# Last layer's middle norm: residual turned inside the last y group, next weights in places of their own, first token tile's products ahead of the second tile's norm

## The chip, the cores and the metric

The kernel runs on one NeuronCore of a Trainium2 chip. Its engines run side by side and wait for each other by semaphores: PE (TensorE, matrix products and transposes into PSUM), DVE (VectorE), ACT (ScalarE), POOL (GpSimd) and SP, which here issues DMA transfers. The metric is device time in microseconds (us); lower is better.

## The reference, cut to what matters

A two-layer backbone: 256 tokens, width 1024, float32. Layer 0 mixes by attention, layer 1 by a state-space scan (SSD); each is followed by a norm, a squared-ReLU MLP of width 4096 and another norm. The change lies in layer 1, at the norm between mixer and MLP:

```
y_lat = finish(z_l, x_l, yl_f, flip(yl_b))            # ends in  y @ w_out   (2048 -> 1024)
h_lat = layer_norm(ALPHA*h_lat + g_m_l*y_lat, ln_mix_g[i], ln_mix_b[i])
f_lat = squared_relu_mlp(h_lat*(1 + sc_f_l) + sh_f_l, ff_w1[i], ff_w2[i])
h_lat = layer_norm(ALPHA*h_lat + g_f_l*f_lat, ln_ff_g[i], ln_ff_b[i])
```

## The kernel before

**Precision.** Every large product keeps float32 precision by splitting both operands into a high and a low part and adding three products (h·h, l·h, h·l). Weights come from memory as float32 in transfers of 1 MB (`raw`, two buffers, `emit_w`, L47 to L62), each holding two units. For each unit ACT casts the high half (`wh`, two casts of 128x512, L61) and DVE subtracts to get the low half (`wl`, L62). Only four `wh`/`wl` pairs exist (pool `wsp`), so a cast waits until PE has read the unit four places earlier, and a transfer waits until both units of the `raw` two places earlier are converted. `next_w` emits up to two units ahead.

**Order.** A scheduler of the tile framework places the instructions: inside each engine they may stand in another order than the source writes them. The engine then works through its list in that order. SP's list holds nearly all transfers.

**The stage of the change** is the second half of `layer1` (L1007 on). The SSD runs in four groups of heads; the last, `ssd(3)`, is woven with `so()`, the products of w_out for blocks k = 0 to 11. The products for k = 12 to 15 follow after the group, tile of 128 tokens by tile (`i`), half of 512 columns by half (`h`): 12 matmuls each, four sets, in the PSUM tiles so00, so01, so10, so11. The residual lies transposed in `X[0]`; 16 PE transposes (`xr`, L1060) and four ACT copies turn it into `Xt`, here between the halves. `add_half` (L277) multiplies by the gate, adds and takes the half's statistics on DVE; `ln_mid` (L298) forms the moments, normalises the tile in one DVE instruction (L302), turns it back with 8 PE transposes (`ut`, L308) and splits it into `u4h` and `u4l` for each of the eight k blocks.

Then comes the MLP. The first four of its 32 hidden blocks are computed with tokens as rows (`f1r`, 24 matmuls of 512 columns for each token tile, over weight units 140 to 143), relu and square (`rr`), and four transposes back (`rt`, L383). The others (`f1a`, 24 matmuls of 256 columns for each block) go the usual way. The second product `f` (w2, `down`) follows after each eight blocks. Three PSUM banks, "aux", serve xr, ut, f1r, rt and f1a in turn. The two rows of the norm's gain and bias (`mixg`, `mixb`) and the two of the last norm (`ffg`, `ffb`) are broadcast transfers of 512 KB; ACT scales the first two (L1097), DVE applies them to `Xt` (L1102).

Of the kernel before, what the change touches and what calls it, by code (L numbers as in the profile page):

```python
# [39 lines left out]
class Net:  # L40
# [217 lines left out]

    def row(self, r, nm):

        t = self.tk.tile([128, 1024], F32, tag="row", name=nm, bufs=4)
        self.nc.sync.dma_start(t, self.a["rows"][r, :].partition_broadcast(128))
        return t

    def down(self, acc, lh, ll, w, k, last, tiles=(0, 1), halves=(0, 1)):

        mm = self.nc.tensor.matmul
        wh, wl = w
        for i in tiles:
            for h in halves:  # L270
                c = slice(512 * h, 512 * h + 512)
                ps = acc[i][h]
                mm(ps, lh(i), wh[:, c], start=(k == 0), stop=False)  # L273
                mm(ps, ll(i), wh[:, c], start=False, stop=False)  # L274
                mm(ps, lh(i), wl[:, c], start=False, stop=last)  # L275

    def add_half(self, acc, i, h, g, x, st):  # L277

# [19 lines left out]
    def ln_mid(self, i, x, st, aff, uh, ul):  # L298

        nc = self.nc  # L300
        mv = self.moments(st, f"lm1{i}")
        nc.vector.tensor_scalar(x, x, mv[:, 0:1], mv[:, 1:2], op0=ALU.subtract, op1=ALU.mult)  # L302
        c = slice(128 * i, 128 * i + 128)
        for q in range(2):
            pt = self.bank("aux", f"ut{i}{q}")
            for m in range(4):
                k = 4 * q + m
                nc.tensor.transpose(pt[:, 128 * m:128 * m + 128], x[:, 128 * k:128 * k + 128], self.ident)  # L308
            for m in range(4):
                k = 4 * q + m  # L310
                p = pt[:, 128 * m:128 * m + 128]
                sc, sh = aff[:, 0, k:k + 1], aff[:, 1, k:k + 1]
                nc.scalar.activation(uh[k][:, c], p, AF.Identity, bias=sh, scale=sc)
# [5 lines left out]
                nc.vector.tensor_sub(ul[k][:, c], t, uh[k][:, c].bitcast(F32))  # L319

    def ln_out(self, i, x, st, g, b):
        nc = self.nc
# [52 lines left out]
    def hidden_rows(self, i, ps, fs):  # L375
# [4 lines left out]
        nc.vector.tensor_mul(r, r, r)  # L380
        pt = self.bank("aux", f"rt{i}")
# [490 lines left out]
    def ssm_in(self, g, uh, ul):  # L872
# [19 lines left out]
        xw = [sp.tile([128, 2, 512], F32, tag=f"xw{d}", name=f"xw{g}{d}") for d in range(2)]  # L892
# [119 lines left out]
    def layer1(self):  # L1012
# [9 lines left out]
        self.sT = self.cst.tile([128, 2, 192], F32, name="sT")  # L1022
        self.aneg = self.cst.tile([128, 1], F32, name="aneg")
        nc.scalar.activation(self.aneg, self.vec("alog"), AF.Exp)
        with tc.tile_pool(name="dq", bufs=1, space=DRAM) as dqp:
            dq = dqp.tile([2, 64, 256], F32, name="dq")
            self.dq = dq
            with tc.tile_pool(name="sp", bufs=2) as sp:
                self.sp = _Multi(tc, sp, dict(cy=2, ct=1, B=1, C=2, xt0=2, xt1=2, xw0=1, xw1=1, Bt=1, xc=1,
                                              cf=2, cb=2, S0=1, S1=1, A=2, E=2, W=2))  # L1030
                for j in range(NZ):
                    self.z_tile(j, uh, ul)
# [4 lines left out]
                acc = [[self.bank("mm", f"so{i}{h}") for h in range(2)] for i in range(2)]  # L1037
                st = lambda y, k: (lambda i: y[k % 8][:, 256 * (k // 8) + 128 * i:256 * (k // 8) + 128 * i + 128])

                def so():  # L1040
                    for k in range(12):
                        self.down(acc, st(yh, k), st(yl, k), self.next_w(whole=True), k, False)
                        yield
                self.weave(self.ssd(3, yh, yl), so())
        aff = self.affine("affm1", self.vec("mixg")[:, 8:16], self.vec("mixb")[:, 8:16], (0,),
                          mT[:, :, 32:40], mT[:, :, 24:32])
        u4h, u4l = self.new_act("u4")
        with tc.tile_pool(name="tk", bufs=1) as self.tk, tc.tile_pool(name="fp1", bufs=2) as fp:
            X = self.tk.tile([128, 2, 1024], F32, name="Xt")
            ws = [self.next_w(whole=True, ahead=0) for _ in range(4)]  # L1050
            bn = [self.stat_tile(f"bm{i}") for i in range(2)]
            for i in range(2):
                for h in range(2):
                    for k in range(12, 16):
                        self.down(acc, st(yh, k), st(yl, k), ws[k - 12], k, k == 15, (i,), (h,))
                    if h == 0:
                        for q in range(2):
                            pt = self.bank("aux", f"xr{i}{q}")
                            for m in range(4):
                                nc.tensor.transpose(pt[:, 128 * m:128 * m + 128],  # L1060
                                                    self.X[0][:, 4 * q + m, 128 * i:128 * i + 128], self.ident)
                            nc.scalar.copy(X[:, i, 512 * q:512 * q + 512], pt)
                    self.add_half(acc, i, h, self.gates[2], X[:, i, :], bn[i])
                self.ln_mid(i, X[:, i, :], bn[i], aff, u4h, u4l)

            self.fp = _Multi(tc, fp, dict(fh=9, fl=9, r=2, q=2))
            pair = lambda m: tuple(self.fp.tile([128, 256], F32R, tag=t, name=f"f1{t}{m}") for t in ("fh", "fl"))
            ws = [self.next_w(whole=True) for _ in range(4)]
            first = [pair(m) for m in range(4)]
            for i in range(2):  # L1070
                ps = self.bank("aux", f"f1r{i}")
                c = slice(128 * i, 128 * i + 128)
                for k in range(8):
                    wh, wl = (w[:, 512 * (k % 2):512 * (k % 2) + 512] for w in ws[k // 2])
                    nc.tensor.matmul(ps, u4h[k][:, c], wh, start=(k == 0), stop=False)
                    nc.tensor.matmul(ps, u4l[k][:, c], wh, start=False, stop=False)
                    nc.tensor.matmul(ps, u4h[k][:, c], wl, start=False, stop=(k == 7))
                self.hidden_rows(i, ps, first)
            acc = [[self.bank("mm", f"f1{i}{h}") for h in range(2)] for i in range(2)]
            ag, ab = self.row(2, "mixg1"), self.row(3, "mixb1")  # L1080
            fg, fb = self.row(4, "ffg1"), self.row(5, "ffb1")
            for c in range(4):
                fs = [] if c else list(first)
                for m in range(len(fs), 8):
                    w = self.next_w()
                    fh, fl = pair(m)
                    ps = self.bank("aux", f"f1a{m}")[:, :256]
                    self.gemm(ps, w, u4h, u4l, 0, 256)
                    self.hidden(ps, 0, 256, fh, fl)
                    fs.append((fh, fl))  # L1090
                lh = lambda m: (lambda i: fs[m][0][:, 128 * i:128 * i + 128])
                ll = lambda m: (lambda i: fs[m][1][:, 128 * i:128 * i + 128])
                for m in range(8 if c < 3 else 4):
                    self.down(acc, lh(m), ll(m), self.next_w(whole=True), 8 * c + m, False)
                if c == 1:
                    for t in (ag, ab):
                        nc.scalar.activation(t, t, AF.Copy, scale=ALPHA)  # L1097
                    for i in range(2):
                        for t, op in ((ag, ALU.mult), (ab, ALU.add)):
                            for h in range(2):  # L1100
                                x = X[:, i, 512 * h:512 * h + 512]
                                nc.vector.tensor_tensor(x, x, t[:, 512 * h:512 * h + 512], op=op)  # L1102
            ws = [self.next_w(whole=True) for _ in range(4)]
            bn = [self.stat_tile(f"bf{i}") for i in range(2)]
            for i in range(2):
                for h in range(2):
                    for m in range(4, 8):
                        self.down(acc, lh(m), ll(m), ws[m - 4], 24 + m, m == 7, (i,), (h,))
                    self.add_half(acc, i, h, self.gates[5], X[:, i, :], bn[i])
                self.ln_out(i, X[:, i, :], bn[i], fg, fb)  # L1110

    def chain(self, *gs):
        for g in gs:
# [96 lines left out]
```

## Time and profile before

| what | value |
|---|---|
| time, three runs | 1177.57, 1180.91, 1181.55 us; median 1180.91 |
| the profiled execution | 1180.05 us; its span 1178.3 us, so 1.75 us lie around the span |
| PE busy | 1120.6 us (95%), 6976 matmuls; weight loads 911.6 us (77%) |
| DVE, ACT busy | 838.2 us (71%), 603.3 us (51%) |
| chain that ended last | PE 80%, DVE 8%, DMA 6%, ACT 5% |

Times in the rows below are microseconds from the start of the span. "Busy" says nothing by itself about what a wait costs; in this stage it matters which wait ends last before PE goes on. Ends of matmuls are modelled, so the distance between starts is their rate.

### The profile page before, as it was taken

How to read it: one execution, taken by the hardware profiler on the slowest of the kernel's cores; microseconds unless marked ns; L12 is line 12 of the kernel's file. 1: busy time of each engine (PE TensorE's matmuls, PEld its weight loads, DVE VectorE, ACT ScalarE, POOL GpSimd, SP SyncE). 2: the span in 40 equal slices, each digit the busy share in tenths (PEclk: the TensorE clock that was granted, in tenths of full speed). 3: DMA queues.
4: the chain of work that ended last, by engine and by line, in shares of the span. 5: the costliest groups of instructions: out<-in, count | busy, mean ns of one | idle time of the engine just before them, and what ended most of it. 6: DMA issues, size and time to landing. Idle time of an engine off the chain costs nothing.

```text
span 1178.3 us, 18541 instructions
## 1 busy us (share of the span) xinstructions
PE 1120.6 (95%) x6976; PEld 911.6 (77%) x6976; DVE 838.2 (71%) x1701; ACT 603.3 (51%) x1382; POOL 48.2 (4%) x79
## 2 busy tenths in 40 slices
PE   6999999998999999999999898999999996999996
PEld 4777767977978878878898776767777675898895
DVE  4499885867949667764435888979897768565566
ACT  4377776145422312322314647787878856454551
POOL 1200000022000000000001400000000000000000
PEclk8999999998999999999999999999999998999998
DMA  8833342522636466752322125435455563455551
GB/s 326 310 126 125 108 145 87 173 100 74 202 118 221 148 209 225 256 192 72 107 72 73 53 105 153 152 108 179 145 168 150 199 214 112 175 183 195 195 179 72
DMA packets 41433, 182.79 MB, mean 155 GB/s; under 512 B 4608, under 2 KB 5248, under 8 KB 28288
## 3 DMA queue, kind: packets, MB, share of 16 engines
q1 hardware_dynamic: 41056, 181.36, 45.9%
q8 instruction: 55, 0.90, 0.3%
q10 hardware_dynamic: 288, 0.26, 0.1%
q14 instruction: 34, 0.28, 0.1%
HBM read 180.41 MB, written 1.18 MB: 154 GB/s over the span
## 4 chain that ended last, share of the span: by engine, by line
PE 80%; DVE 8%; DMA 6%; ACT 5%; issue 1%; SPq 0%; DVEq 0%; ACTq 0%
PE f0a L87 5%; PE f0a L88 5%; PE f0a L89 5%; PE f0b L87 5%; PE f0b L89 5%; PE f0b L88 5%; PE y L983 3%; PE f L275 2%; PE f L274 2%; PE f L273 2%; PE f1a L89 2%; PE f1a L87 2%; PE f1a L88 2%; PE q L78 2%; DMA wm<-in_w_mod 2%; PE x L89 2%
## 5 line engine op out<-in xcount | busy, mean ns | idle before, releaser
L61 ACT CAST wh<-raw 128x512 fp32r<-128x512 f32 x404 | 237.8, 620 | 392.9 <-PE f0b L88 125.9
L62 DVE TENSOR_TENSOR wl<-raw,wh 128x512 fp32r<-128x512 f32 x404 | 268.5, 687 | 118.5 <-ACT wh L61 117.6
L87 PE MATMUL f0a<-u1h,wh 128*128 128x512 f32 (+1 forms) x320 | 112.7, 354 | 1.5 <-ACT u1h L193 1.5
L87 PE MATMUL f0b<-f0fh,wh 128*128 128x512 f32 (+1 forms) x320 | 113.8, 356 | 0.0
L89 PE MATMUL f0a<-u1h,wl 128*128 128x512 f32 (+1 forms) x320 | 112.1, 351 | 0.0
L88 PE MATMUL f0a<-u1l,wh 128*128 128x512 f32 (+1 forms) x320 | 112.0, 352 | 0.0
L89 PE MATMUL f0b<-f0fh,wl 128*128 128x512 f32 (+1 forms) x320 | 111.7, 349 | 0.0
L88 PE MATMUL f0b<-f0fl,wh 128*128 128x512 f32 (+1 forms) x320 | 110.9, 347 | 0.1
L150 DVE SCALAR_TENSOR_TENSOR ma<-wm,cs,ma 128x1024 f32<-128x1024 f32 x70 | 88.7, 1281 | 22.4 <-DMA wm<-in_w_mod 22.3
L87 PEld LDWEIGHTS f0a<-u1h,wh 128*128 128x128 f32 x320 | 61.6, 193 | 11.8 <-ACT u1h L193 2.3
L89 PEld LDWEIGHTS f0b<-f0fh,wl 128*128 128x128 f32 x320 | 60.2, 188 | 10.4 <-issue 2.1
L87 PEld LDWEIGHTS f0b<-f0fh,wh 128*128 128x128 f32 x320 | 60.1, 188 | 10.4 <-issue 2.6
L89 PEld LDWEIGHTS f0a<-u1h,wl 128*128 128x128 f32 x320 | 61.8, 193 | 8.0 <-issue 0.4
L88 PEld LDWEIGHTS f0b<-f0fl,wh 128*128 128x128 f32 x320 | 60.1, 188 | 9.6 <-issue 1.4
L88 PEld LDWEIGHTS f0a<-u1l,wh 128*128 128x128 f32 x320 | 61.6, 193 | 7.7 <-issue 0.4
L87 PE MATMUL f1a<-u4h,wh 128*128 128x256 f32 x224 | 63.5, 284 | 0.0
L89 PE MATMUL f1a<-u4h,wl 128*128 128x256 f32 x224 | 63.4, 283 | 0.0
L88 PE MATMUL f1a<-u4l,wh 128*128 128x256 f32 x224 | 63.4, 283 | 0.0
L87 PE MATMUL x<-u2h,wh 128*128 128x512 f32 x128 | 51.2, 400 | 2.2 <-DVE cy L794 2.2
L967 ACT ACTIVATE W<-A,sT 128x128 f32<-128x128 f32 (+1 forms) x128 | 50.2, 458 | 5.7 <-DMA A<-dq 3.1
L89 PE MATMUL x<-u2h,wl 128*128 128x512 f32 x128 | 51.2, 401 | 0.3 <-DVE wl L62 0.3
L361 DVE SCALAR_TENSOR_TENSOR X<-f0b,mT,X 128x256 f32<-128x256 f32 x48 | 21.0, 478 | 42.8 <-PE f0b L89 42.8
(435 smaller groups left out, 2724.8 us busy)
## 6 DMA issues: line engine op xcount, KB each, us to landing
raw<-in_wall SPq DMA_DIRECT2D x102, 1024.0 KB, 5.0
wm<-in_w_mod SPq DMA_DIRECT2D x96, 512.0 KB, 4.4
A<-dq SPq DMA_DIRECT2D x32, 256.0 KB, 4.5
E<-dq SPq DMA_DIRECT2D x32, 256.0 KB, 4.9
X<-in_xT SPq DMA_DIRECT2D x8, 256.0 KB, 8.3
gate<-in_rows SPq DMA_DIRECT2D x2, 512.0 KB, 12.8
out_dram<-Xt SPq DMA_DIRECT2D x4, 256.0 KB, 2.0
mixg<-in_rows SPq DMA_DIRECT2D x1, 512.0 KB, 5.9
```

Source lines behind the costliest of these rows:

```text
L61: nc.scalar.copy(h, src[:, c])
L62: nc.vector.tensor_sub(l, src[:, c], h.bitcast(F32))
L78: self.mm = lambda *a, **k: self.tc.keep_in_program_order(self.nc.tensor.matmul(*a, **k))
L87: mm(ps, wh[:, k, :], ah[k][:, c0:c1], start=(k == 0), stop=False)
L88: mm(ps, wh[:, k, :], al[k][:, c0:c1], start=False, stop=False)
L89: mm(ps, wl[:, k, :], ah[k][:, c0:c1], start=False, stop=(k == 7))
L150: nc.vector.scalar_tensor_tensor(t, wm, c, t, op0=ALU.mult, op1=ALU.add)
L273: mm(ps, lh(i), wh[:, c], start=(k == 0), stop=False)
L274: mm(ps, ll(i), wh[:, c], start=False, stop=False)
L275: mm(ps, lh(i), wl[:, c], start=False, stop=last)
L967: nc.scalar.activation(W[:, h, o:o + l1 - l0], A[:, h, l0:l1], AF.Relu, scale=-1.0, bias=self.sT[:, st, r + h:r + h + 1])
L983: mm(ps[64 * a:64 * a + 64, l0:l1], lh[:, hc:hc + 64], mv, start=(n == 0), stop=(n == 5))
```

## The change

Five edits, all around the middle norm of layer 1:

1. The 16 transposes of the residual and their copies move into `so()`, four after each of the odd k from 5 to 11, into a tile that takes the place of `xw` (which gets a pool of its own).
2. The first three of the four weight units of the token-row products (140 to 142) get places of their own, six buffers of the tag "row", and are converted before the norms. The fourth is taken as usual, after the last split of tile 0.
3. The token-row products of tile 0 stand in the source before `ln_mid` of tile 1.
4. Their transposes `rt` follow later, after hidden blocks 4 and 5.
5. The four row transfers move behind the second product of the second eight blocks in the source; they use the "row" places that the weights leave.

The core of the diff:

```
-        t = self.tk.tile([128, 1024], F32, tag="row", name=nm, bufs=4)
+        t = self.tk.tile([128, 1024], F32, tag="row", name=nm, bufs=6)
...
+    def res_rows(self, x, i, q):
+        pt = self.bank("aux", f"xr{i}{q}")
+        for m in range(4):
+            nc.tensor.transpose(pt[:, 128 * m:128 * m + 128], self.X[0][:, 4 * q + m, 128 * i:128 * i + 128], self.ident)
+        nc.scalar.copy(x[:, 512 * q:512 * q + 512], pt)
...
+                        if k % 2 and k > 3:
+                            i, q = divmod((k - 5) // 2, 2)
+                            self.res_rows(X[i], i, q)
...
+            for n in range(3):
+                wh, wl = (self.tk.tile([128, 1024], F32R, tag="row", name=f"f1w{n}{p}", bufs=6) for p in "hl")
+                self.emit_w(self.wpos, [(wh[:, 512 * q:512 * q + 512], wl[:, 512 * q:512 * q + 512]) for q in range(2)])
...
-                self.ln_mid(i, X[:, i, :], bn[i], aff, u4h, u4l)
+                if i:
+                    with tc.issue_after(turned[0].ins), tc.issue_after(turned[1].ins):
+                        first_w.append(self.next_w(whole=True, ahead=0))
+                    rows.append(f1_rows(0))
+                turned = self.ln_mid(i, X[i], bn[i], aff, u4h, u4l)
+            rows.append(f1_rows(1))
...
+                    if c == 0 and m < 6:
+                        self.rows_turn(m - 4, rows[m - 4], first)
```

What this does to the engines' lists, at three places. **PE, from the end of so11.** Before, tile 1's transposes (ut10, ut11) stood ahead of every f1r product; names end in running numbers:

```order
L275 MATMUL so11_9136<-wl139_9600,yh7_6515 128x512
L308 MATMUL ut10_9747<-con_78,Xt_9590 128x128 x4
L308 MATMUL ut11_9768<-con_78,Xt_9590 128x128 x4
L1075 MATMUL f1r0_9839<-wh140_9791,u4h0_9568 128x512
L1076 MATMUL f1r0_9839<-wh140_9791,u4l0_9576 128x512
```

Now tile 0's transposes follow the last so11 product, and tile 1's stand inside tile 0's products:

```order
L1091 MATMUL f1r0_9782<-f1w0l_9634,u4h1_9598 128x512
L1089 MATMUL f1r0_9782<-f1w1h_9641,u4h2_9599 128x512
L1090 MATMUL f1r0_9782<-f1w1h_9641,u4l2_9607 128x512
L1091 MATMUL f1r0_9782<-f1w1l_9642,u4h2_9599 128x512
L1089 MATMUL f1r0_9782<-f1w1h_9641,u4h3_9600 128x512
L316 MATMUL ut10_9815<-con_78,Xt1_9538 128x128 x2
L1090 MATMUL f1r0_9782<-f1w1h_9641,u4l3_9608 128x512
```

So ten products of tile 0 no longer wait for the second norm. **DVE, from the last weight unit of w_out (139) to the normalisation of tile 0**, now (before, no weight unit stood between wl139 and that normalisation, `Xt<-Xt,lm10mv`):

```order
L62 TENSOR_TENSOR f1w0l_9634<-raw140_9635,f1w0h_9633 128x512 x2
L62 TENSOR_TENSOR f1w1l_9642<-raw140_9635,f1w1h_9641 128x512 x2
L290 TENSOR_TENSOR gt00_9677<-so00_9136,gate2_90 128x512
L291 TENSOR_TENSOR Xt0_9381<-Xt0_9381,gt00_9677 128x512
L290 TENSOR_TENSOR gt01_9693<-so01_9137,gate2_90 128x512
L292 BN_STATS bm0_9663<-Xt0_9381 128x6
L62 TENSOR_TENSOR f1w2l_9648<-raw142_9649,f1w2h_9647 128x512 x2
L291 TENSOR_TENSOR Xt0_9381<-Xt0_9381,gt01_9693 128x512
L290 TENSOR_TENSOR gt10_9756<-so10_9138,gate2_90 128x512
L292 BN_STATS bm0_9663<-Xt0_9381 128x6
L291 TENSOR_TENSOR Xt1_9538<-Xt1_9538,gt10_9756 128x512
L298 BN_AGGR lm10mv_9697<-bm0_9663 128x2
```

Six weight conversions, two of them from the transfer raw142, now stand ahead of tile 0's last steps. **ACT, after the last splits of tile 1**, now (before, the two scalings of the rows stood far earlier, among the casts of y):

```order
L321 ACTIVATE u4h7_9604<-ut11_9836,affm1_9591 128x128
L324 ACTIVATE ut_9854<-ut11_9836,affm1_9591 128x128
L1127 ACTIVATE mixg1_10713<-mixg1_10713 128x1024
L1127 ACTIVATE mixb1_10715<-mixb1_10715 128x1024
L388 ACTIVATE rr1_9882<-f1r1_9857 128x512
L61 CAST wh147_9957<-raw146_9903 128x512 x2
L378 ACTIVATE r_9938<-f1a4_9913 128x256
```

The scalings, which need the row transfers, stand ahead of the relu of f1r1. On SP the four row transfers moved too: mixg and mixb from behind raw136 to behind raw146, ffg and ffb from behind raw138 to behind raw148.

## Rows read from the trace of the kernel before

**Rows 1.** Waits of PE: engine line waited for, total us, times, longest us.
```profile
PE ut L308 <- DVE Xt L302: 7.3, 1, 7.3
PE rt L383 <- DVE rr L380: 3.2, 2, 1.8
```

**Rows 2.** Windows of 20 us: width, busy us of each engine, PEclk, DMA share, GB/s.
```profile
980.00:1000.00 20.00, 15.68 (x62) 12.54 (x63) 17.05 (x40) 11.44 (x27) 0.00 (x0) 0.83 0.25 83
1140.00:1160.00 20.00, 20.00 (x117) 17.64 (x116) 11.95 (x22) 9.74 (x20) 0.00 (x0) 1.00 0.40 145
```

**Rows 3.** Chain that ended last, 930 to 1012 us: start us, us, what.
```profile
959.89 0.23 PE so L273
...
962.62 0.87 PE xr L1060 x8
...
981.09 1.94 PE ut L308 x8
983.03 0.43 PE f1r L1075
```

**Rows 4.** Windows of 1 us around two falls of the clock; columns as in Rows 2.
```profile
976.00:977.00 1.00, 0.00 (x0) 0.00 (x0) 0.94 (x4) 1.00 (x4) 0.00 (x0) 0.79 1.00 426
...
986.00:987.00 1.00, 1.00 (x5) 0.77 (x4) 1.00 (x5) 0.68 (x3) 0.00 (x0) 0.59 0.47 197
...
92.00:93.00 1.00, 1.00 (x9) 0.95 (x8) 1.00 (x5) 0.97 (x3) 0.00 (x0) 0.77 0.00 0
...
95.00:96.00 1.00, 1.00 (x4) 0.73 (x4) 1.00 (x5) 0.32 (x1) 0.00 (x0) 0.53 0.00 0
```

**Rows 5.** Timeline of PE: start us, us, instruction, [idle before <-releaser].
```profile
91.18 1.24 PE L79 MATMUL pt<-con,P 128*128 128x128 f32 x8 [2.05 <-DVE P L499]
...
999.74 0.65 PE L383 MATMUL rt<-con,rr 128*128 128x128 f32 x4 [1.81 <-DVE rr L380]
1000.83 0.28 PE L89 MATMUL f1a<-u4h,wl 128*128 128x256 f32 x1
1001.55 0.28 PE L89 MATMUL f1a<-u4h,wl 128*128 128x256 f32 x1
...
1011.75 0.39 PE L273 MATMUL f<-wh,f1fh 128*128 128x512 f32 x1
```

**Rows 6.** Timeline of DVE in the norm of tile 0, same columns.
```profile
968.51 0.21 DVE L290 BATCH_NORM_AGGREGATE lm10mv<-bm 128x2 f32<-128x12 f32 x1
...
969.75 0.80 DVE L302 TENSOR_SCALAR Xt<-Xt,lm10mv 128x1024 f32<-128x1024 f32 x1
970.47 1.89 DVE L62 TENSOR_TENSOR wl<-raw,wh 128x512 fp32r<-128x512 f32 x3
972.28 0.40 DVE L318 TENSOR_SCALAR ut<-ut,affm 128x128 f32<-128x128 f32 x1
```

**Rows 7.** Timeline of ACT in the same norm, same columns.
```profile
969.48 2.18 ACT L61 CAST wh<-raw 128x512 fp32r<-128x512 f32 x4 [0.43 <-PE so L274]
971.57 0.45 ACT L313 ACTIVATE u4h<-ut,affm 128x128 fp32r<-128x128 f32 x1
...
973.20 0.46 ACT L313 ACTIVATE u4h<-ut,affm 128x128 fp32r<-128x128 f32 x1
973.55 0.45 ACT L316 ACTIVATE ut<-ut,affm 128x128 f32<-128x128 f32 x1
```

**Rows 8.** Issue of raw142 on SP; then issues by line: KB each, median us to landing.
```profile
961.73 0.33 SPq L51 DMA_DIRECT2D raw<-in_wall  x1
...
raw<-in_wall SPq DMA_DIRECT2D x15, 1024.0 KB, 5.0
...
mixg<-in_rows SPq DMA_DIRECT2D x1, 512.0 KB, 5.9
mixb<-in_rows SPq DMA_DIRECT2D x1, 512.0 KB, 6.7
...
gate<-in_rows SPq DMA_DIRECT2D x2, 512.0 KB, 12.8
```

More of the change, by code (lines that the diff above doesn't have):

```diff
@@ L312, in ln_mid @@
                 sc, sh = aff[:, 0, k:k + 1], aff[:, 1, k:k + 1]
-                nc.scalar.activation(uh[k][:, c], p, AF.Identity, bias=sh, scale=sc)
+                a = nc.scalar.activation(uh[k][:, c], p, AF.Identity, bias=sh, scale=sc)
                 t = self.tk.tile([128, 128], F32, tag="ut", name="ut", bufs=4)
@@ L318, in ln_mid @@
                     nc.vector.tensor_scalar(t, p, sc, sh, op0=ALU.mult, op1=ALU.add)
-                nc.vector.tensor_sub(ul[k][:, c], t, uh[k][:, c].bitcast(F32))
+                v = nc.vector.tensor_sub(ul[k][:, c], t, uh[k][:, c].bitcast(F32))
+        return a, v
     def ln_out(self, i, x, st, g, b):
@@ L373, in hidden, with rows_sq @@
         nc.vector.tensor_sub(fl[:, c0:c1], q[:, :n], fh[:, c0:c1].bitcast(F32))
-    def hidden_rows(self, i, ps, fs):
+    def rows_sq(self, i, ps):
         nc = self.nc
@@ L380, in hidden_rows, with rows_turn @@
         nc.vector.tensor_mul(r, r, r)
+        return r
+    def rows_turn(self, i, r, fs):
+        nc = self.nc
         pt = self.bank("aux", f"rt{i}")
@@ L891, in ssm_in @@
         G["xt"] = [sp.tile([128, 2, 512], F32, tag=f"xt{d}", name=f"xt{g}{d}") for d in range(2)]
-        xw = [sp.tile([128, 2, 512], F32, tag=f"xw{d}", name=f"xw{g}{d}") for d in range(2)]
+        xw = [self.xwp.tile([128, 2, 512], F32, tag=f"xw{d}", name=f"xw{g}{d}") for d in range(2)]
         Bt = sp.tile([128, 2, 128], F32, tag="Bt", name=f"Bt{g}")
@@ L1038, in layer1 @@
                 st = lambda y, k: (lambda i: y[k % 8][:, 256 * (k // 8) + 128 * i:256 * (k // 8) + 128 * i + 128])
+                X = []
                 def so():
@@ L1042, in so @@
                         self.down(acc, st(yh, k), st(yl, k), self.next_w(whole=True), k, False)
+                        if k % 2 and k > 3:
+                            i, q = divmod((k - 5) // 2, 2)
+                            if q == 0:
+                                X.append(self.xwp.tile([128, 1024], F32, tag=f"xw{i}", name=f"Xt{i}"))
+                            self.res_rows(X[i], i, q)
                         yield
@@ L1048, in layer1, with f1_rows @@
         with tc.tile_pool(name="tk", bufs=1) as self.tk, tc.tile_pool(name="fp1", bufs=2) as fp:
-            X = self.tk.tile([128, 2, 1024], F32, name="Xt")
             ws = [self.next_w(whole=True, ahead=0) for _ in range(4)]
+            first_w = []
+            for n in range(3):
+                wh, wl = (self.tk.tile([128, 1024], F32R, tag="row", name=f"f1w{n}{p}", bufs=6) for p in "hl")
+                self.emit_w(self.wpos, [(wh[:, 512 * q:512 * q + 512], wl[:, 512 * q:512 * q + 512]) for q in range(2)])
+                self.wpos += 1
+                self.wout += 1
+                first_w.append((wh, wl))
+            self.fp = _Multi(tc, fp, dict(fh=9, fl=9, r=2, q=2))
+            pair = lambda m: tuple(self.fp.tile([128, 256], F32R, tag=t, name=f"f1{t}{m}") for t in ("fh", "fl"))
+            first = [pair(m) for m in range(4)]
+            def f1_rows(i):
+                ps = self.bank("aux", f"f1r{i}")
+                c = slice(128 * i, 128 * i + 128)
+                for k in range(8):
+                    wh, wl = (w[:, 512 * (k % 2):512 * (k % 2) + 512] for w in first_w[k // 2])
+                    nc.tensor.matmul(ps, u4h[k][:, c], wh, start=(k == 0), stop=False)
+                    nc.tensor.matmul(ps, u4l[k][:, c], wh, start=False, stop=False)
+                    nc.tensor.matmul(ps, u4h[k][:, c], wl, start=False, stop=(k == 7))
+                return self.rows_sq(i, ps)
             bn = [self.stat_tile(f"bm{i}") for i in range(2)]
+            rows = []
             for i in range(2):
@@ L1055, in layer1 @@
                         self.down(acc, st(yh, k), st(yl, k), ws[k - 12], k, k == 15, (i,), (h,))
[L1056 to L1063, printed above, removed]
-                self.ln_mid(i, X[:, i, :], bn[i], aff, u4h, u4l)
[L1066 to L1078, printed above, removed]
+                    self.add_half(acc, i, h, self.gates[2], X[i], bn[i])
+                if i:
[4 more added lines that the diff above has]
+            rows.append(f1_rows(1))
             acc = [[self.bank("mm", f"f1{i}{h}") for h in range(2)] for i in range(2)]
-            ag, ab = self.row(2, "mixg1"), self.row(3, "mixb1")
-            fg, fb = self.row(4, "ffg1"), self.row(5, "ffb1")
             for c in range(4):
@@ L1095, in layer1 @@
                 if c == 1:
+                    ag, ab = self.row(2, "mixg1"), self.row(3, "mixb1")
+                    fg, fb = self.row(4, "ffg1"), self.row(5, "ffb1")
                     for t in (ag, ab):
@@ L1108, in layer1 @@
                         self.down(acc, lh(m), ll(m), ws[m - 4], 24 + m, m == 7, (i,), (h,))
-                    self.add_half(acc, i, h, self.gates[5], X[:, i, :], bn[i])
-                self.ln_out(i, X[:, i, :], bn[i], fg, fb)
+                    self.add_half(acc, i, h, self.gates[5], X[i], bn[i])
+                self.ln_out(i, X[i], bn[i], fg, fb)
     def chain(self, *gs):
```

6 lines of the change are left out of this document (4 added, 2 removed).

## The prediction, before the run

> **What bounds the kernel now.** I read the waits of PE first, then the windows, then the chain and the timelines of the stage. PE's two waits in this stage, 7.3 us for tile 1's normalised rows and 3.2 us in two pieces for `rr`, are the largest that the change can touch [rows 1]. In the window from 980 to 1000 us PE is busy 15.7 of 20 us, at 0.83 of its clock; from 1140 to 1160 it is busy throughout at full clock [rows 2]. So what follows this stage is bound by PE, and a microsecond saved here should arrive at the end.
>
> The stretch to compare runs from the first product of so00, 959.73 us, to the first product `f`, 1011.75 us [rows 5]: 52.0 us. (The chain writes that first product as 959.89 [rows 3]; I subtract the 0.16 by which its starts run behind the timeline's.) PE's own work in it at full clock: 12 products take 962.62 − 959.89 = 2.73 us [rows 3], so the 48 of so and the 48 of f1r take 21.8; eight transposes take 0.87 [rows 3], so 40 (xr, ut, rt) take 4.4; six f1a products take 1001.55 − 1000.83 = 0.72 [rows 5], so 96 take 11.5. Together 37.7 us. The other 14.3 are stalls and slow clock: 10.5 from the two waits [rows 1], about 2.8 because PE ran slow from 981.1 to 986.8 (eight transposes in 1.94 us instead of 0.87 [rows 3]; then nine products of 0.43 [rows 3] instead of 0.23), and a rest of 1.
>
> **The change, part by part.** Times are on the scale of the trace before.
>
> *Residual turned early.* All 16 transposes, 4 × 0.44 = 1.8 us, now stand ahead of so00, where PE is already full: so00 starts at 961.5. Nothing is won or lost by this in itself, since 1.8 us leave the later part. The sets end at 964.2, 967.0, 969.7 and 972.4. The four ACT copies (one cast's length, 0.52 by rows 7) lie beside the products of so, which lead their weights by more than that; I count 0, or +0.5 if one of them delays the SSD's last `W`.
>
> *Weights ahead of the norm.* In the program raw142 may only start when unit 139 is converted, and that unit's cast waits for block k = 11. Three of the four transpose groups stand ahead of k = 11's end, so the issue moves from 961.73 [rows 8] to 963.1; landing takes 5.0 [rows 8], to 968.1. ACT then casts unit 142 (0.52 each: 971.57 − 969.48 over four [rows 7]), DVE subtracts (0.60 each: 972.28 − 970.47 over three [rows 6]), done at 969.7. Behind it DVE has four instructions of 0.60 (the order shows them) before the moments: 972.1. From the moments to the normalised tile before took 970.55 − 968.51 = 2.0 [rows 6]; one more statistic adds 0.3: 974.4. PE, which ended so11 at 972.4, waits 2.1 us here, where it had no such wait. Cost of the ready weights: these 2.1 us.
>
> *Tile 0's products ahead of the second norm.* The first split stands 0.9 us behind the transposes' start, 12 splits of 0.35 follow (973.55 − 973.20 [rows 7]), one square root of 0.35 between them: 974.5 + 0.9 + 4.55 = 979.95. Unit 143 stands behind them on ACT: two casts to 981.0, the last subtract to 981.7, f1r0 ends at 982.1. PE's own work, eight transposes and 24 products (6.3 us), would end no earlier than 981.8, so it fits under the splits. Tile 1's normalisation on DVE runs meanwhile; the 7.3 us go.
>
> *Tile 1's products.* ACT's list from 981.0 on: 12 splits (4.2), six casts (3.1), the relu rr0 (0.52) to 988.8; the last product follows at 989.4. ACT sets the pace, not PE (988.2). The remaining 19 f1a products of hidden block 4 (five stand inside f1r1) and rt0 end at 992.2. rt0's relu and square are long done: the first piece of the 3.2 us goes.
>
> *The rows, moved.* This is the added wait. mixg's transfer needs the place of unit 140, which f1r1's block k = 1 reads last, at 984.8; issued at 984.9, landing after 5.9 [rows 8] at 990.8, mixb (issued 0.4 later, 6.7) at 992.0. ACT is ready at 988.8 but must scale both rows first (1.0 each, two casts' length): 993.0, and only then comes the relu rr1, 993.6. Behind it on ACT stand unit 147, the relus of f1a and all splits of rt0. Who waits: hidden block 5 uses the PSUM bank of f1r1 and starts at 993.7, a new stall of 1.5 us. It runs 2.9 us to 996.6, rt1 and three products `f` to 997.8. Hidden block 6 uses block 5's bank and waits for its relu, which stands behind three casts of 0.52 and seven short copies after unit 147, about 998.4: 0.6 us more. Blocks 6 and 7 end at 1004.2, with 0.7 us of `f` already done. The 14 remaining DVE and ACT instructions on `Xt` lie beside PE's full stretch [rows 2]: 0.
>
> **Sum.** `f` stands as if it had started at 1003.5 instead of 1011.75: 8.25 us won. One term is open, the clock. The new gap of 2.1 us is like the one of 2.05 before 91.18 [rows 5], after which the clock was low from 92.5 to 95.9 [rows 4]; the gap of 1.81 before 999.74 [rows 5] left no trace on it. A fall of 3.4 us halves PE's rate for as long: up to 1.7 us, as f1r0 has only 0.3 us in hand. I take half, 0.85: 7.4 us won. The profiled execution's 1180.05 becomes 1172.65. The median of the runs, 1180.91, is 0.86 above it, so on that scale 1173.5.
>
> The Trainium skill (TensorE: Matmul & The Clock Gate, Terms) prices a throttled stretch at its length times the share of pulses left out. Here it lasted from 976.6 to 986.8 [rows 4], 10.2 us, and by that rule would be worth 5.1 us; the rows give 2.8, because PE idled through the first half. By the page the sum would be 1171.2; I keep the rows.
>
> **Rivals.**
>
> *More is won.* None of the three new stalls appears (2.1, 1.5, 0.6) and the clock stays high: raw142 lands early because no row transfers share the engines then, and mixg is there before ACT asks. For it: 4.2 us of my stalls rest on landing times of other moments. Against: DVE's four instructions behind unit 142 are there at any landing time. Up to 1180.91 − 8.25 − 4.2 = 1168.5; typically 1169.7.
>
> *The order does not overlap as written.* If tile 0's products are held behind the second norm after all (by the splits on ACT or the late unit 143), only the 3.2 us [rows 1] and a piece of the slow clock come: 3 to 4 us, 1177.4. Against: the PE order shows ten products ahead of ut10.
>
> *Slower: the row transfers hold ACT.* One mechanism, at one place: mixg and mixb now stand on ACT ahead of rr1. At a landing of 12.8 us, which the same kind of transfer took once (`gate` [rows 8]), mixg lands at 997.7, mixb at 998.5, rr1 ends at 1000.1 and block 5 starts 6.5 us later than I have it. PE would be idle for some 8 us, and the clock would fall as it did in the 7.3 us gap, 2.8 us more: 1173.5 + 9.3 = 1182.8. It decides against the change from a landing of about 12 us; mixg alone took 5.9 [rows 8].
> That a waiting instruction holds those behind it is what the Trainium skill (TensorE: Matmul & The Clock Gate, Architectural detail) states for ACT and DVE, strict first in, first out; no row here isolates it for ACT. By that rule the 1.5 us stand; without it they would not, and the time would be 1172.0.
>
> *Half of the gain.* Late raw142 (the stall of 2.1 grows us by us), a full fall of the clock and rows of 8 us: 1176.5 to 1180.
>
> **Chances.** Forecast (1171.3 to 1176) 0.60; more won 0.17; half 0.12; no overlap 0.05; slower 0.06. 0.3% of the time is 3.5 us, about what a measurement of this kernel tells from no change: faster means below 1177.4. Forecast, more won and half of "half" give 0.83; same 0.12; slower 0.05, as part of the slow case ends within the bound. The range leaves out the far tail of "more" and the cases above 1178: 1169 to 1178.
>
> **What would show it.** After the change the wait of PE for the second norm must be gone and tile 0's f1r products must start before tile 1's transposes. A wait of PE of about 2 us before ut00, ended by DVE's normalisation, and before it a wait of DVE for unit 142; a wait of ACT for mixg or mixb of about 2 us, and one of PE before block 5 of 1 to 2 us, ended by rr1's relu. The clock is to be read in the 10 us from ut00 on. It is wrong if PE waits over 4 us at one of these places, or if the windows after block 7 show PE less than full.

## The result, and the profile after

Five runs of the changed kernel took 1171.28 to 1174.77 us, median 1173.0; five of the kernel before 1176.42 to 1181.55, median 1180.2. The ratio is 0.9947, with a 95% interval of 0.9924 to 0.9970. The forecast was 1173.5. The profiled execution after took 1171.94 us, its span 1170.2.

Executions differ by several microseconds ahead of this stage: the last square `ysq` of the SSD starts between 942.4 and 949.6 us in the traces shown here. So I measure the stage by a stretch that both kernels share: from that last `ysq` to the end of the span. ACT's last two `ysq`, before:

```profile
936.94 0.42 ACT L989 ACTIVATE ysq<-X 128x256 f32<-128x256 f32 x1
...
945.78 0.42 ACT L989 ACTIVATE ysq<-X 128x256 f32<-128x256 f32 x1 [2.86 <-DVE X L987]
```

and after, with the transposes of the residual that now stand between them on PE:

```profile
936.15 0.42 ACT L1002 ACTIVATE ysq<-X 128x256 f32<-128x256 f32 x1
938.19 0.60 PE L282 MATMUL xr<-con,X 128*128 128x128 f32 x4
945.53 0.42 ACT L1002 ACTIVATE ysq<-X 128x256 f32<-128x256 f32 x1 [3.01 <-DVE X L1000]
```

From there to the end it is 1178.3 − 945.78 = 232.5 us before and 1170.2 − 945.53 = 224.7 after: 7.85 us less. Below, this number is called the measure. Positions are given from `ysq` too, as [+28.1].

The measure flatters the change. One of the four early transpose groups stands ahead of the last `ysq` and delays it: from the `ysq` before, it comes 9.38 us later after, 8.84 before. The measure leaves about this much out for every kernel with the early residual. Counted from the `ysq` before, the stage takes 241.36 us before and 234.05 after, and 7.3 us are won.

Waits of PE in the stage after (line waited for, total us, times, longest), to set beside [rows 1]:

```profile
PE ut L316 <- DVE Xt L310: 1.9, 1, 1.9
PE f1r L1089 <- ACT rr L388: 0.8, 1, 0.8
PE f1r L1090 <- DVE u4l L327: 0.6, 2, 0.3
PE ut L316 <- ACT ut L324: 0.5, 1, 0.5
PE f1a L87 <- ACT r L378: 0.2, 1, 0.2
```

The 7.3 and the 3.2 us are gone; 4.0 us in five groups have come. The windows (busy us of PE, PEld, DVE, ACT, POOL; clock; DMA share; GB/s), beside [rows 2, 4]:

```profile
980.00:1000.00 20.00, 18.19 (x108) 14.53 (x108) 17.93 (x43) 18.02 (x42) 0.00 (x0) 1.00 0.75 264
1140.00:1160.00 20.00, 20.00 (x89) 16.40 (x88) 13.12 (x24) 5.37 (x11) 0.00 (x0) 1.00 0.15 53
974.00:975.00 1.00, 0.89 (x8) 0.65 (x6) 0.96 (x3) 0.46 (x1) 0.00 (x0) 1.00 0.00 0
```

ACT is busy 18.0 of the 20 us where it was 11.4, PE 18.2 where it was 15.7, and the clock is 1.00 throughout, also behind the new gap. Later PE is full, as before. PE's timeline of the stage, beside [rows 3, 5]:

```profile
960.57 0.48 PE L273 MATMUL so<-wh,yh 128*128 128x512 f32 x1
...
971.35 0.39 PE L275 MATMUL so<-wl,yh 128*128 128x512 f32 x1
973.67 1.06 PE L316 MATMUL ut<-con,Xt 128*128 128x128 f32 x8 [1.94 <-DVE Xt L310]
...
983.07 0.40 PE L1091 MATMUL f1r<-wl,u4h 128*128 128x512 f32 x1
984.29 0.50 PE L1089 MATMUL f1r<-f1w0h,u4h 128*128 128x512 f32 x1 [0.83 <-ACT rr L388]
...
991.18 0.39 PE L1091 MATMUL f1r<-wl,u4h 128*128 128x512 f32 x1
...
998.47 0.39 PE L87 MATMUL f1a<-u4h,wh 128*128 128x256 f32 x1 [0.18 <-ACT r L378]
...
1004.33 0.39 PE L273 MATMUL f<-wh,f1fh 128*128 128x512 f32 x1
```

Rows 960.57 to 971.35 are the products of so; 973.67 is ut00 and ut01; 983.07 the last product of f1r0, 984.29 and 991.18 the first and the last of f1r1; 998.47 the first of hidden block 6; 1004.33 the first of the long row of `f`, three of which are already done. What DVE does ahead of ut00, beside [rows 6]:

```profile
962.81 1.29 DVE L62 TENSOR_TENSOR f1w0l<-raw,f1w0h 128x512 fp32r<-128x512 f32 x2 [0.63 <-ACT f1w0h L61]
...
967.75 1.28 DVE L62 TENSOR_TENSOR f1w2l<-raw,f1w2h 128x512 fp32r<-128x512 f32 x2
...
972.72 0.81 DVE L310 TENSOR_SCALAR Xt<-Xt,lm10mv 128x1024 f32<-128x1024 f32 x1
```

and ACT, beside [rows 7, 8]: 967.03 is the landing of raw142, then two splits of tile 0 and the scaling of the rows:

```profile
967.03 1.14 ACT L61 CAST f1w2h<-raw 128x512 fp32r<-128x512 f32 x2 [2.69 <-DMA raw<-in_wall]
...
978.54 0.46 ACT L321 ACTIVATE u4h<-ut,affm 128x128 fp32r<-128x128 f32 x1 [0.48 <-DVE ut L326]
...
980.17 0.46 ACT L321 ACTIVATE u4h<-ut,affm 128x128 fp32r<-128x128 f32 x1 [0.48 <-DVE ut L326]
...
989.99 1.06 ACT L1127 ACTIVATE mixg<-mixg 128x1024 f32<-128x1024 f32 x1
991.77 1.06 ACT L1127 ACTIVATE mixb<-mixb 128x1024 f32<-128x1024 f32 x1 [0.71 <-DMA mixb<-in_rows]
992.73 0.58 ACT L388 ACTIVATE rr<-f1r 128x512 f32<-128x512 f32 x1
```

### The profile page after: what moved, and what is told of

The parts are those of the page before. It is cut to its first block, busy times and chain, and to the rows that moved or that the text cites. A ratio compares the mean times of both kernels' runs of the same rounds, so it can differ in the third digit from the quotient of the medians.

```text
span 1170.2 us, 18528 instructions
## 1 busy us (share of the span) xinstructions
PE 1120.9 (96%) x6976; PEld 908.6 (78%) x6976; DVE 837.6 (72%) x1701; ACT 603.0 (52%) x1382; POOL 48.3 (4%) x79
## 3 DMA queue, kind: packets, MB, share of 16 engines
q1 hardware_dynamic: 41056, 181.36, 46.4%
## 4 chain that ended last, share of the span: by engine, by line
PE 79%; DVE 8%; DMA 6%; ACT 5%; issue 1%; DVEq 0%; SPq 0%; ACTq 0%
PE f0a L87 5%; PE f0a L88 5%; PE f0a L89 5%; PE f0b L87 5%; PE f0b L89 5%; PE f0b L88 5%; PE y L996 3%; PE f L275 2%; PE f L274 2%; PE f L273 2%; PE f1a L87 2%; PE f1a L89 2%; PE f1a L88 2%; PE q L78 2%; DMA raw<-in_wall 2%; PE x L89 2%
## 5 line engine op out<-in xcount | busy, mean ns | idle before, releaser
L61 ACT CAST wh<-raw 128x512 fp32r<-128x512 f32 x398 | 234.0, 620 | 386.0 <-PE f0b L88 126.7
L62 DVE TENSOR_TENSOR wl<-raw,wh 128x512 fp32r<-128x512 f32 x398 | 264.9, 688 | 112.3 <-ACT wh L61 108.9
L87 PE MATMUL x<-u2h,wh 128*128 128x512 f32 x128 | 51.3, 401 | 2.2 <-DVE cy L807 2.2
L89 PE MATMUL x<-u2h,wl 128*128 128x512 f32 x128 | 51.2, 401 | 0.3 <-DVE wl L62 0.3
L88 PE MATMUL x<-u2l,wh 128*128 128x512 f32 x128 | 50.8, 397 | 0.0
```

Of the source, the lines that this page charges most:

```text
L61: nc.scalar.copy(h, src[:, c])
L62: nc.vector.tensor_sub(l, src[:, c], h.bitcast(F32))
L87: mm(ps, wh[:, k, :], ah[k][:, c0:c1], start=(k == 0), stop=False)
L88: mm(ps, wh[:, k, :], al[k][:, c0:c1], start=False, stop=False)
L89: mm(ps, wl[:, k, :], ah[k][:, c0:c1], start=False, stop=(k == 7))
```

## Experiments

Diffs are against the changed kernel (224.7) unless said otherwise. All were run once with a profile and judged by the measure; e10, e11, c3 and c4 were also timed. One trace cannot tell a few tenths of a microsecond from chance: mixb alone landed in 4.9 to 6.1 us in five kernels that issue it alike (after, e2, e6, e11, c3). From e3 on, the clock is at 1.00 in this stage unless said otherwise.

**One edit undone at a time.** Theory A: the order of tile 0's products is what pays; rival B: the early weights are.

*e1: f1_rows(0) behind tile 1's norm.*

```
-                    rows.append(f1_rows(0))
                 turned = self.ln_mid(i, X[i], bn[i], aff, u4h, u4l)
+            rows.append(f1_rows(0))
             rows.append(f1_rows(1))
```

> Undoes edit 3 alone: tile 0's 24 token-row products stand in the source behind tile 1's norm again; weights stay early, rt late, residual early. PE's list becomes ut00, ut01, ut10, ut11, then all of f1r0. The measure for all runs is the time from the last square of the SSD (the last ysq on ACT) to the end of the span: 232.5 us before, 224.7 after, so 7.8 is what the five edits won there (0.36 more if the one transpose group ahead of that square is counted). Theory A (the overlap of f1r0 with the second norm carries the gain, as the prediction has it): 4 us or more come back, 228.7 or more, with a wait of PE of 3 us or more for tile 1's rows or splits and a fall of the clock. Rival B (the weights being ready carries it, the overlap only shifts work that the splits on ACT and DVE pace anyway): 3 us or less come back, at most 227.7.

*e8: no early weights; all four units by `next_w` at the later place.*

```
-            for n in range(3):
-                wh, wl = (self.tk.tile([128, 1024], F32R, tag="row", ...
...
-                        first_w.append(self.next_w(whole=True, ahead=0))
+                    first_w += [self.next_w(whole=True, ahead=0) for _ in range(4)]
```

> Undoes edit 2 alone: the four units 140 to 143 are taken from the usual four pairs, after tile 0's splits begin; products of tile 0 still stand ahead of the second norm, rt late, residual early. Theory A: DVE has six conversions less ahead of tile 0's norm, so the wait before ut00 (1.9 us after) goes, and the conversions then stand among the splits; at most 2 us come back, 226.7 or less. Rival B: 4 us or more come back, 228.7 or more, with PE waiting for wh or wl of f1r0.

Measured: e1 228.8 (+4.1), e8 228.9 (+4.2). PE's waits in e1:

```profile
PE ut L316 <- ACT u4h L321: 3.3, 1, 3.3
PE f1r L1089 <- ACT ut L324: 2.0, 1, 2.0
PE ut L316 <- DVE Xt L310: 2.0, 1, 2.0
```

and in e8:

```profile
PE ut L316 <- DVE Xt L310: 2.1, 1, 2.1
PE f1r L1084 <- DVE u4l L327: 1.4, 3, 0.7
PE f1r L1085 <- DVE wl L62: 1.4, 1, 1.4
```

A was right on e1 and wrong on e8, B the reverse: neither theory holds alone. The two edits need each other. Without the order the weights lie ready and unused; without the weights tile 0's products start, then wait for a `wl` (1.4), and the second norm ends late (2.1, now at ut10). In both the clock fell to 0.50, in e1 from 977 to 987, in e8 twice for some 3 us. So the 4 us mix two things; e9 below separates them for e1, and nothing does for e8. Edit 5 was not undone by itself.

*e2: the transposes rt at once.*

```
+                self.rows_turn(i, self.rows_sq(i, ps), first)
...
-                    if c == 0 and m < 6:
-                        self.rows_turn(m - 4, rows[m - 4], first)
```

> Undoes edit 4 alone: the transposes rt0 and rt1 stand in the source right behind the token-row products, ahead of hidden blocks 4 to 7. rt0 falls among the products of f1r1, rt1 behind them. Theory: PE waits for rr1 (relu on ACT behind the scaling of mixg, then the square on DVE) by 2 to 2.5 us before rt1; 226.7 to 227.2. Rival: ACT's backlog paces the following blocks in any case, and less than 0.7 us come back, 225.4 or less.

Measured 226.4 (+1.7), between the two ranges. PE waits 1.5 us for rr1, as before the change. Some of the 1.7 is the clock: behind the same gap of 1.94 us as after it fell here, for some 3 us, and the eight transposes took longer:

```profile
974.08 1.90 PE L316 MATMUL ut<-con,Xt 128*128 128x128 f32 x8 [1.94 <-DVE Xt L310]
```

*e3: the residual turned between the halves, as before.*

```
-                            self.res_rows(X[i], i, q)
...
+                    if h == 0:
+                        for q in range(2):
+                            self.res_rows(X[i], i, q)
```

> Undoes edit 1 alone: the 16 transposes of the residual and their copies stand between the halves of the last products again. Theory: PE does the same work on the same full stretch, and the copies on ACT end before DVE is through with the six conversions, so 0 to 0.5 us come back, 224.7 to 225.2 (the square itself starts 0.36 earlier, which makes 225.0 to 225.5). Rival: the copies of tile 1 stand between the splits on ACT, as before the change, and 1.5 us or more come back, 226.2 or more.

Measured 225.2 (+0.5), with the clock at 1.00. But here all four groups of transposes stand behind the last `ysq`, and after only three. Counted from the `ysq` before (935.04 in this trace), e3 takes 234.0 us and after 234.05: the edit by itself wins nothing that these traces show. (The expectations of e1 and e3 name the group ahead of `ysq`; in e1's the sign is wrong, it lessens the win.) In e3 PE waits 1.8 us for ACT's copies of the late residual, and less than after ahead of ut00, 0.65.

**How much of it is the clock.** *e9: e1 with idle transposes in PE's two waits behind ut0 and ut1; nothing reads what they write.*

```
+            if q:
+                fill = self.bank("md", f"fill{i}")
+                for m in range((24, 16)[i]):
+                    nc.tensor.transpose(fill[:, 128 * (m % 4):128 * (m % 4) + 128], x[:, 128 * (m % 8):...], self.ident)
```

> Measure as before. This is e1_norm_first (228.8: both norms ahead of all f1r products) with 24 and 16 idle transposes, written to an unused PSUM bank, on PE behind the transposes of tile 0 and of tile 1; they fill PE's waits of 3.3 and 2.0 us and nothing reads them. Theory C (most of what e1_norm_first loses is the clock, which is 0.50 from 977 to 987.8 there: eight transposes 1.94 instead of 1.06 us and ten products at 0.43 instead of 0.23): the granted clock stays at 1.00 and the measure falls by 2.3 to 2.9, to 225.9 to 226.5, so that the order by itself was worth 1.2 to 1.8 and the clock the rest. Rival A (the order by itself is worth the 4.1): 228.3 or more even with the clock at 1.00.

Measured 227.1: 1.7 us come back from e1's 228.8, less than theory C's 2.3 to 2.9, more than A's 0.5. The fillers stand behind the first gap, and that gap of 1.95 us was enough for a fall (0.50 from 971 to 974.4); the f1r products ran at full rate. So of e1's 4.1 us the clock had at least 1.7, and the order at most 2.4.

*e10: the same on the kernel before: 60 idle transposes in the 7.3 us.*

```
+                if i:
+                    fill = self.bank("md", "fill")
+                    for m in range(60):
+                        c = slice(128 * (m % 8), 128 * (m % 8) + 128)
+                        nc.tensor.transpose(fill[:, 128 * (m % 4):128 * (m % 4) + 128], X[:, 0, c], self.ident)
                 self.ln_mid(i, X[:, i, :], bn[i], aff, u4h, u4l)
```

> Measure as before; the kernel before has 232.5. Here the kernel before gets 60 idle transposes on PE, written to an unused PSUM bank and read by nothing, in its wait of 7.3 us for tile 1's normalised rows; nothing else is changed. Theory C (PE's slow clock from 981.1 to 986.8 cost the kernel before 2.8 us, as rows of its trace price it): the clock holds, and the measure is 229.5 to 230.3. The page's rule (Trainium skill, TensorE: Matmul & The Clock Gate, Terms) prices the throttled 10.2 us at 5.1: 227.4. Rival A (behind the wait PE is paced by its weights or by the splits, so the clock costs nothing): 232 to 232.7.

Measured 229.97, 2.55 us less than before; timed, 1176.3 us against 1177.88, ratio 0.9986 (0.9978 to 0.9995). That is 1.6 us, by the interval 0.6 to 2.6, so the 2.55 of the one trace lies at the upper end. Windows of 981 to 986, before:

```profile
981.00:986.00 5.00, 4.91 (x16) 4.27 (x17) 5.00 (x13) 2.72 (x7) 0.00 (x0) 0.50 0.48 170
```

and e10, with PE's timeline of the place:

```profile
981.00:986.00 5.00, 5.00 (x26) 4.14 (x24) 5.00 (x14) 3.85 (x10) 0.00 (x0) 1.00 0.63 213
```

```profile
972.78 6.71 PE L1068 MATMUL fill<-con,Xt 128*128 128x128 f32 x60
980.26 1.07 PE L308 MATMUL ut<-con,Xt 128*128 128x128 f32 x8 [0.77 <-DVE Xt L302]
```

Products of f1r start every 0.23 us there, and every 0.43 before, because PE was kept busy with nothing. (The counts, 26 and 16, are not of the same work: eight of the 16 are transposes.) Theory C holds; its size, 2.8 by the rows, agrees with the trace. The rule of the Trainium skill (TensorE: Matmul & The Clock Gate, Terms) would have given 5.1; the trace does not agree, since PE had no work in the first half of the slow stretch.

**Taking the new waits away, one by one.**

*e4: the early low halves on POOL (`sub` is POOL's subtraction for the three early units).*

```
-            nc.vector.tensor_sub(l, src[:, c], h.bitcast(F32))
+            (sub or nc.vector.tensor_sub)(l, src[:, c], h.bitcast(F32))
```

> Measure: time from the last ysq of the SSD to the end of the span; the changed kernel has 224.7. Here the six subtractions that make the low halves of the three early units run on POOL instead of DVE. Theory A (DVE's queue, not the landing of raw142, sets PE's new wait of 1.9 us before ut00): DVE loses 3.9 us of work ahead of tile 0's normalisation, the wait shrinks to under 0.3 us, the splits start 1.9 earlier, and the measure is 222.5 to 223.2. Rival B (the wait follows the landing of the early units, or what comes later is bound by ACT's own list anyway): the wait may go, but the measure stays at 224.2 or more.

Measured 224.5. The transposes ut00 start at [+26.3] instead of [+28.1]: theory A is right on what sets that start. The wait itself shrinks only to 1.2, since five products of so11 now stand behind ut00. The time is B's. The gain is given back at ut10 (0.8 us for the second norm) and in f1r1, which waits 1.0 for a `u4h` and ends at [+47.7], after 45.9, with more products of block 4 inside it.

*e6: f1r1 in the idle PSUM bank.*

```
-                ps = self.bank("aux", f"f1r{i}")
+                ps = self.bank(("aux", "md")[i], f"f1r{i}")
```

> Measure as before, the changed kernel has 224.7. Here tile 1's products f1r1 accumulate in a PSUM bank that is idle in this stage, instead of the bank of f1r0. Theory A: the wait of 0.8 us of PE for rr0's relu is on the path, and goes: 223.7 to 224.1. Rival B: f1r1 is paced by the splits on ACT behind it, so that the 0.8 comes back as longer waits for u4l: 224.4 to 224.8.

Measured 224.5: B's time. The 0.8 is gone and PE is through with rt1 at [+51.2], 0.9 earlier. But hidden block 6 starts at [+52.9] as it did after. ACT, e6:

```profile
991.16 1.06 ACT L1127 ACTIVATE mixg<-mixg 128x1024 f32<-128x1024 f32 x1
993.77 1.06 ACT L1127 ACTIVATE mixb<-mixb 128x1024 f32<-128x1024 f32 x1 [1.54 <-DMA mixb<-in_rows]
994.74 0.58 ACT L388 ACTIVATE rr<-f1r 128x512 f32<-128x512 f32 x1
```

ACT now waits 1.54 us for mixb, with the relus behind it in its list, and not for the slow splits that B named. It came to mixg where it did after ([+44.4] and [+44.5]), and mixb was issued at the same place; but mixb took 6.1 us to land, after 5.3, so that rr1's relu starts 0.8 us later. Whether the edit or chance made this landing longer, one trace does not show, so e6 decides for neither theory.

*e7: all copies t of the split by ACT.*

```
-                if m % 2:
-                    nc.scalar.activation(t, p, AF.Identity, bias=sh, scale=sc)
-                else:
-                    nc.vector.tensor_scalar(t, p, sc, sh, op0=ALU.mult, op1=ALU.add)
+                nc.scalar.activation(t, p, AF.Identity, bias=sh, scale=sc)
```

> Measure as before, the changed kernel has 224.7. Here all sixteen copies t in the split of the normalised rows are made by ACT; DVE no longer reads PSUM there. In the changed kernel a pair of k takes 1.63 us, of which ACT waits 0.48 for DVE's read of the same bank. Theory A (that alternation sets the pace): a pair takes four ACT instructions of 0.355, 1.42 us; eight pairs win up to 1.7, some of it ahead of f1r0's end only: 223.3 to 224.2. Rival B (ACT's whole list sets the pace, its waits being slack that the casts and relus fill): ACT gets eight instructions more, 2.8 us, of which the waits hide half: 225 to 226.

Measured 224.6, between the two ranges. ACT's splits run without a gap:

```profile
975.10 0.46 ACT L321 ACTIVATE u4h<-ut,affm 128x128 fp32r<-128x128 f32 x1
975.45 0.46 ACT L323 ACTIVATE ut<-ut,affm 128x128 f32<-128x128 f32 x1
975.79 0.47 ACT L321 ACTIVATE u4h<-ut,affm 128x128 fp32r<-128x128 f32 x1
976.13 0.48 ACT L323 ACTIVATE ut<-ut,affm 128x128 f32<-128x128 f32 x1
976.47 0.48 ACT L321 ACTIVATE u4h<-ut,affm 128x128 fp32r<-128x128 f32 x1
```

A pair of k takes 976.47 − 975.10 = 1.37 us, so the alternation did set the pace. But the scheduler then put ut10 behind all of f1r0, and PE waits 0.8 there and 0.8 for a cast of unit 143 instead; and block 6 starts at [+52.8].

*e11: rows scaled and applied behind block 7; c3: that and e6's bank; c4: c3 and e4's POOL.*

```
+                    with tc.issue_after(seventh[0].ins), tc.issue_after(seventh[1].ins):
                         for t in (ag, ab):
                             nc.scalar.activation(t, t, AF.Copy, scale=ALPHA)
```

> Measure: time from the last ysq of the SSD to the end of the span; the changed kernel has 224.7. Here ACT's scaling of mixg and mixb, and DVE's products with them, stand behind hidden block 7, so that neither engine waits for these transfers ahead of the relu of f1r1. Theory D (in the changed kernel, and with the experiments that took one wait each away, the landing of mixb sets when hidden block 6 may start, but PE reaches it only 0.2 to 0.4 us earlier): 224.2 to 224.5 alone. Rival E (the transfers have nothing to do with it): 224.6 to 224.8.

> Measure as before; the changed kernel has 224.7, with tile 1's products in a bank of their own 224.5, where PE finished the products on rt1 1.0 us before hidden block 6 could start. Here that bank and the later scaling of the rows together. Theory D: what the bank frees is no longer held by the rows, and comes through: 223.3 to 223.7. Rival E: block 6 is held by something else (its own weights, the relu of block 5), 224.3 to 224.6.

> Measure as before. The previous kernel with the early units' low halves on POOL as well, which alone gave 224.5 and took 0.7 us off the wait ahead of ut00. Theory D: that too comes through now, 222.6 to 223.2. Rival F (tile 1's splits on ACT set the pace of f1r1 whatever starts earlier): no better than the previous kernel, 223.3 to 223.8, with longer waits of PE for u4h or u4l in f1r1.

| kernel | measure | rt1 done | block 6 starts | median of timed runs | ratio to before (95%) |
|---|---|---|---|---|---|
| after | 224.67 | +52.1 | +52.9 | 1173.0 | 0.9947 (0.9924 to 0.9970) |
| e6, bank alone | 224.53 | +51.2 | +52.9 | one run | |
| e11, rows later alone | 224.57 | +52.1 | +52.9 | 1169.99 | 0.9947 (0.9929 to 0.9964) |
| c3, both | 223.91 | +51.3 | +52.0 | 1169.74 | 0.9940 (0.9927 to 0.9952) |
| c4, both and POOL | 224.38 | +50.8 | +52.7 | 1170.54 | 0.9945 (0.9933 to 0.9957) |

The timed runs of the last three stand beside a median of 1177.88 for the kernel before, those of after beside 1180.2; only the ratios compare. Each alone gives 0.1 us, both together 0.76; e11 and c3 both lie between the ranges of D and E. One half of theory D's interplay is borne out: taking the rows out of ACT's way wins nothing in e11, and with them out of the way the bank wins a further 0.66 us. The other half, that the bank alone wins nothing, rests on e6 with its late mixb and is not shown. In c3 PE's last gap is still 0.26 us, for the relu of block 5. c4 was to be 222.6 to 223.2 or no better than c3; it is worse than c3, and block 6 comes later again though rt1 is done earlier. There ACT waits for weights that took 7.7 us to land (the median of such transfers after is 4.9), with the relus of blocks 4 and 5 behind them:

```profile
992.85 0.62 ACT L61 CAST wh<-raw 128x512 fp32r<-128x512 f32 x1 [1.75 <-DMA raw<-in_wall]
```

So c4 does not say what its edit is worth. c3 is the best version by the trace; its timed gain over before is clear, but from the changed kernel the intervals can't tell it.

Not tried: the rows in places of their own, so that they land early.

## Why the prediction was right, and where two errors met in it

The forecast and its side were right, and so was the main mechanism: the 7.3 us wait for the second norm went, because tile 0's products fill it. That the number came out so close was luck, as the steps show. Positions are from `ysq` (the forecast's times less 945.78); the last column adds the 0.54 us by which the change delays `ysq`, and is the one to set beside the forecast:

| step | forecast | after | after, from the same start |
|---|---|---|---|
| so00 starts | +15.7 | +15.0 | +15.6 |
| wait before ut00 | 2.1 | 1.9 | 1.9 |
| f1r0's last product ends | +36.3 | +37.8 | +38.3 |
| f1r1's last product ends | +43.6 | +45.9 | +46.4 |
| rr1's relu ends | +47.8 | +47.8 | +48.3 |
| wait before block 5, block 6 | 1.5, 0.6 | 0, 0.2 | 0, 0.2 |
| `f`, counted from its first product | +57.7 | +58.1 | +58.6 |
| the clock's fall | 0.85 | 0 | 0 |

- **The residual** was put at nothing won, and that is what the traces show (e3): PE has no gap there, and so00 starts as much later as forecast.
- **The new wait before ut00** came in the size worked out, but not quite for the reason given. The forecast, and its sign, was that DVE waits for unit 142, so that the landing of raw142 sets the end. DVE waited for nothing: it has no pause from 962.81 to 973.5 and came to unit 142 at 967.75, about 0.2 us behind the first of ACT's two casts. Its own list sets the wait, and e4 shows that taking the six subtractions off it moves ut00. Landing and list nearly tied, so the size came out either way.
- **The splits were mis-sized.** I gave each 0.35 us by two neighbouring rows of ACT, 1.05 a pair of k. A pair takes 980.17 − 978.54 = 1.63, of which 0.48 is ACT's wait for DVE's read of the same PSUM bank (e7 shows it: without that read the wait is gone). The rows of one group of four did not show this wait; a whole tile's splits, first to last, would have: in the trace before, ACT waits 0.66 us for DVE's read at 979.40.
- **A wait was missed.** f1r1 takes the bank of f1r0 and waits 0.8 for rr0's relu (e6). With the splits this makes f1r1 2.8 us late.
- **The stall before block 5 did not come**, though rr1's relu came only 0.5 us later than I had it: ACT did wait for mixb with the relu behind it, but 0.7 us and from a later start, since its own splits were late; and mixb took 5.3 to land where I took 6.7. PE was late too, so nobody waited for rr1. My two errors had opposite sides: 2.8 us too few up to f1r1, 1.9 too many behind it.
- **The clock** stayed up, so the 0.85 us put down for it was not spent; it paid for the 0.9 us by which `f` was late. 8.25 − 0.9 is the 7.3 us that were won, where the forecast had 8.25 − 0.85. The even odds were somewhat high: at this place eight traces have a gap of 1.88 to 2.10 us, and the clock fell in two of them (1.94 in e2, 1.95 in e9; not in after, e1, e6, e7, e11, c3). That the old fall cost 2.8 us was right within 0.3 in the one trace of e10 (2.55); its timed runs give 0.6 to 2.6.

So where do the 7.3 us come from? 2.55 are the slow clock that the kernel before paid behind its 7.3 us of idling, by e10's trace. The other 4.8 are what the five edits win beside the clock: the kernel before with its clock held is still that much slower. The edits' shares do not add up: nothing for the residual and 1.7 for the late rt (with some clock in it) stand beside 4.1 for the order of tile 0's products, or 4.2 for the early weights (both with clock in them), each lost when either is undone.

Of the rivals, "more is won" was nearest: two of its three stalls stayed away, but their room was taken by f1r1's delay. "The row transfers hold ACT" was right on the place and wrong on the size: in the chain of waits after, the landing of mixb stands on the path,

```profile
986.43 5.26 DMA mixb<-in_rows
991.77 1.07 ACT mixb L1127
```

yet e11 takes it off and wins 0.1 us. PE itself is that close ahead of it: in e11 it goes from rt1 through `f` to block 6 without a marked wait, and block 6 starts where it did after.

## What to carry to other kernels

When a stage ends with several lists close together (here PE's own products, ACT's splits, a landing), the chain names only the last of them; taking it away wins no more than the distance to the next (e11: 0.1 us), and the next removal is to be tried on top of it (c3: 0.66 more, in one trace). Before a difference of tenths between two single traces is put down to an edit, compare the landings in them. And let a measure start ahead of everything that the change moves, or moved work counts as won. Price a step that two engines share from its first to its last row over a whole tile, not from two neighbouring rows. And before a long wait is credited with its full length, look at the clock behind it: a part of the price can be the slow stretch that follows, which harmless filler work shows in one run.

## What the hardware showed beyond that

**POOL blocks some DVE instructions.** In e4, while POOL subtracts, DVE's sum of two SBUF tiles (`Xt<-Xt,gt`) takes 1.44 and 1.60 us, before and behind that 0.69; the product that reads PSUM (`gt<-so,gate`) and the statistics keep their length. DVE:

```profile
964.09 0.69 DVE L290 TENSOR_TENSOR gt<-so,gate 128x512 f32<-128x512 f32 x1 [1.44 <-PE so L275]
964.81 1.44 DVE L291 TENSOR_TENSOR Xt<-Xt,gt 128x512 f32<-128x512 f32 x1
966.28 0.70 DVE L292 BATCH_NORM_STATS2 bm<-Xt 128x6 f32<-128x512 f32 x1
966.89 0.67 DVE L290 TENSOR_TENSOR gt<-so,gate 128x512 f32<-128x512 f32 x1
967.60 1.60 DVE L291 TENSOR_TENSOR Xt<-Xt,gt 128x512 f32<-128x512 f32 x1
```

and POOL:

```profile
963.16 2.54 POOL L62 TENSOR_TENSOR f1w0l<-raw,f1w0h 128x512 fp32r<-128x512 f32 x2 [288.78 <-ACT f1w0h L61]
965.66 3.00 POOL L62 TENSOR_TENSOR f1w1l<-raw,f1w1h 128x512 fp32r<-128x512 f32 x2
968.62 2.98 POOL L62 TENSOR_TENSOR f1w2l<-raw,f1w2h 128x512 fp32r<-128x512 f32 x2
```

The first sum ends 0.59 us behind POOL's change of instruction at 965.66, the second 0.58 behind that at 968.62, as if each began its work only there. The Trainium skill (SBUF — State Buffer, Terms) says that DVE and GpSimd take a shared pair of ports by an exclusive lock held for the whole instruction, so that the loser waits rather than slows down; the trace agrees.

**Two readers of one PSUM bank take turns.** That ACT waits 0.48 us for DVE's read of other columns of the same bank is what the Trainium skill (PSUM — Partial Sum Buffer, PSUM bank collisions raise a hardware error) tells of the compiler: it orders any two accesses of different engines to the same bank and partitions, reads too. The waits after agree, and e7's splits have none of them; the traces do not show what set the order.
